# A decoder trunk on Trainium2: sixteen pairs of up strips, instead of ten, and one pair of gate strips with seven block products for eight

## The chip, the cores and the metric

The kernel runs on one core of a Trainium2 chip. The metric is the device time of one execution in microseconds (us). Engines are named as the profile names them: PE is the matrix engine and PEld its weight load, DVE the vector engine, ACT the scalar engine, POOL the general engine (here it issues the transfers that turn activations), and SP issues the loads of weights.

## The reference, cut to what matters

A trunk of two decoder layers over 256 tokens of width 2048, all in f32. Each layer has an attention mixer, a gated feed-forward part with a causal convolution of width 3, and a gate on a per-layer embedding:

```python
D_MODEL, SEQ, DEPTH = 2048, 256, 2
D_FF = 256 * ((8 * D_MODEL // 3 + 255) // 256)        # 5632
...
def conv_ffn(h, w_up, conv_w, conv_b, w_down):
    u = causal_depthwise_conv(h @ w_up, conv_w, conv_b)
    gate, val = u[..., :D_FF], u[..., D_FF:]
    return (jax.nn.silu(gate) * val) @ w_down
...
# per layer: h += mixer(norm(h)); h += conv_ffn(norm(h)); h += sigmoid(norm(h) @ w_gate) * (p[i] @ w_proj)
```

The up projection is 2048 by 11264 per layer, the down projection 5632 by 2048, the gate 2048 by 2048. With 256 tokens every weight is used for two blocks of 128 tokens.

## The kernel before, in words

**Strips and tiles.** A weight matrix is cut into strips of 512 columns; a strip is computed for both token blocks, each into one PSUM bank of 128x512. Weights arrive as `raw` tiles of 1 MB (128x2048, four blocks of 128x512), loaded on SP's queue into a pool of four (`NRAW`). An f32 block is multiplied as a high and a low part: ACT rounds a tile of two blocks to `whi` (L305), DVE subtracts to get `wlo` (L306), both in pools of four. Each block product is then three matmuls (`add_block`, L342 to L344): low activation by high weight, high by low, high by high. A tile of two blocks for two token blocks is 12 matmuls on PE.

**Seven products for eight.** The class `Seven` takes two strips together. Their first four blocks of 128 rows, two strips and two token blocks form a two by two product of block matrices, each block one tile of two weight blocks. Instead of eight tile products of 6 matmuls each it makes seven (the Strassen-Winograd scheme): `load` brings one raw tile of each strip, `first` to `fourth` make products 1 to 4, and then `fifth`, `sixth` and `seventh` the last three, which add to banks that already hold sums. Per pair it issues 6 matmuls fewer than the plain way. It issues three splits more (seven tiles for four, L464 on ACT and L465 on DVE), four additions of weights on DVE (L458), two copies out of PSUM on ACT (L494 and L502) and four sums in PSUM on DVE (L514 to L517). `block_sums` forms the sums of activations that the scheme needs, once for each set of activations. Its banks are c11, c12, c21 and c22; c11 and c21 belong to the first strip, c12 and c22 to the second.

**Where it stands.** The up projection of each layer is done in two parts; part 1 has pairs 0 to 4, part 2 pairs 5 to 10. A pair is a gate strip (columns of `gate`) and a value strip (columns of `val`), and the two strips of a pair are those of a Seven. Products 1 to 4 of a pair's Seven are put between the tiles of the value strip of the pair before (`begin`; this is called the head below), products 5 to 7 between the tiles of the pair's own first strip (`go_on`), and then the second strip follows (`end`). Before the change every second pair that could be a Seven is one: ten pairs in the two layers. A down projection follows each part, with a Seven for its strips 2 and 3 (four in all). So there are 14 Sevens.

**What follows an up strip.** The strip's two banks are scaled out of PSUM by ACT (`u`, L569), turned by DVE in blocks (L243) and by two transfers on POOL's queue through DRAM (`there`, L246, and `turned`, L254; this is called the turn chain below). One strip later ACT and DVE do the convolution on the turned strip (L935 on ACT, L938 to L944 on DVE); after a gate strip ACT takes SiLU, after a value strip DVE multiplies and splits into `g`, the activations of the down projection.

**What sets the order.** A scheduler places instructions on each engine in the order in which they are written, except that those under `tc.high_priority(offset=...)` (splits, weight additions, sums in PSUM) stand as many places earlier as the offset says, which was 200 for all (`AHEAD`). Each engine works its list in order. The order on each engine is thus known before a run.

The two functions that the change rewrites first, before it:

```python
def go_on(self):                       # tile hooks: product 5 ahead of tile 0, 6 ahead of 1, 7 ahead of 3
    hooks = dict(zip(TAILS, (self.fifth, self.sixth, self.seventh)))
    yield strip_among(self.W, self.strips[0], self.xs, hooks, [self.c11, self.c21], 4, self.base)
```

Of the kernel before, what the change touches and what calls it, by code (L numbers as in the profile page):

```python
# [50 lines left out]
HEADS, TAILS = {8: (1, 3, 5, 7), 6: (1, 2, 4, 5)}, (0, 1, 3)  # L51
# [19 lines left out]
AHEAD = 200  # L71
PI_PARTS = _two_pi_parts()
# [3 lines left out]
def tile_trunk(ctx, tc, head_d, xT_d, x_d, pT_d, pos_d, vec_d, cst_d, csb_d, wqkv, wo_a, wkv, wq_b, wo_b, wup, wdn, wpg, wpp, gfin_d, out_d):  # L76
# [184 lines left out]
    class Turned:  # L261
# [6 lines left out]
        def add(self, s):  # L268
            if self.strip is not None:
                with tc.issue_after(last["square"]), tc.issue_after(last["added"]):  # L270
                    self.use(*self.strip)
            self.strip = (s, turn(s))

        def late(self):
            self.use(*self.strip)

# [44 lines left out]
    def strip_v(W, s, xs, base=0, tail=2, ringed=0, begun=None, ends=True, before=lambda k0: None, room=None, halved=False, ready=None, hooks={}):  # L321
# [8 lines left out]
        for k, o, hi, lo in (g for group in it for g in group):  # L330
# [5 lines left out]
            add_block(ps[o], xs[k], min(o, 1), hi[:, c], lo[:, c], k == 0 and not begun, ends and k == n - 1)  # L336
# [22 lines left out]
    def products(jobs, xs, late=None, at=0, then={}, side=2, seven=None):  # L359
# [7 lines left out]
        if late is not None:  # L367
            n = len(xs)

# [4 lines left out]
            def before(k0):  # L374
                if k0 == at:
                    add()
                if k0 in then:
                    then[k0]()

            hooks = {}  # L380
            if seven is not None:
                tiles = n // 2
                hooks = {tiles - 4: seven.load, tiles - 2: seven.first, tiles - 1: seven.second}
            begun = [
                strip_v(
                    W,
                    s,
                    xs[:n],
                    base,
                    ends=False,  # L390
                    before=before if i == side - 1 else lambda k0: None,
                    room=two_banks() if i == 2 else None,
                    hooks=hooks if i == side - 1 else {},
                )
                for i, (W, s, base) in enumerate(jobs[:side])
            ]
# [5 lines left out]
            hooks = [{0: seven.third}, {0: seven.fourth}] if seven is not None else [{}] * side  # L402
            for b, (W, s, base), more in zip(begun, jobs, hooks):
                yield strip_v(W, s, xs[n:], base + n, begun=b, ready=ready, hooks=more)
                ready = None
            jobs = jobs[side:]
        if seven is not None:
            yield from seven.both()
            jobs = []
        for W, s, base in jobs:  # L410
            yield strip_v(W, s, xs, base)
# [25 lines left out]
    class Seven:  # L437
# [4 lines left out]
        def __init__(self, W, s0, s1, xs, sums, base=0, two=True):  # L442
            self.W, self.strips, self.base, self.two = W, (s0, s1), base, two
            self.xs, self.sums = xs, sums
# [4 lines left out]
        def value_bank(self, o):  # L449
            if not self.two:  # L450
                return bank("values", "acc")
            if o == 0:
                self.banks = two_banks()
            return self.banks[:, o]
# [29 lines left out]
        def first(self):  # L484
            self.c11 = bank("gates")
# [10 lines left out]
        def second(self):  # L496
            self.c12 = self.value_bank(0)
# [6 lines left out]
        def third(self):  # L504
            self.c21 = bank("gates", "acc")
            self.product(self.c21, self.sums[1], self.parts(self.u), True)

        def fourth(self):
            self.c22 = self.value_bank(1)
# [3 lines left out]
            with tc.high_priority(offset=AHEAD):  # L513
# [16 lines left out]

        def go_on(self):
# [3 lines left out]
        def end(self, hooks):  # L535
            return strip_among(self.W, self.strips[1], self.xs, hooks, [self.c12, self.c22], 4, self.base)

        def both(self):
            yield from self.go_on()
            yield self.end({})  # L540
# [681 lines left out]
```

## Time and profile before

| | before |
|---|---|
| three runs | 2280.93, 2282.38, 2282.47 us |
| median | 2282.38 us |
| the profiled execution, whole | 2284.18 us |
| its span in the profile | 2282.4 us |
| granted TensorE clock, mean | 0.998 |
| PE busy | 2267.6 us, 99% of the span |
| DVE busy | 1686.4 us, 74% |
| ACT busy | 1318.8 us, 58% |
| bytes moved | 538.44 MB, 236 GB/s |

A group of the profile stands as line, engine, operation, output and inputs, count, then busy time and mean duration of one. "Idle before" is time in which the engine waited ahead of that group, with what ended the wait. The number of a duration includes some overlap with the next instruction on the same engine, so the step from start to start is shorter than the duration. Instruction counts in the profile can be a few per cent lower than those issued.

### The profile page before, as it was taken

What the parts mean: (1) busy time and instruction counts of PE and PEld (TensorE: products, weight loads), DVE (VectorE), ACT (ScalarE), POOL (GpSimd) and SP (SyncE); (2) the same over time, 40 slices, a digit from 0 to 9 for tenths busy, and PEclk for the clock granted to TensorE, in tenths of its full rate; (3) what the DMA queues carried; (4) which work ended last, traced back from release to release, by engine and by line L of the source; (5) the groups of instructions that cost most, each with busy time, mean ns of one, the idle gap of its engine ahead of it and who ended that gap; (6) DMA issues with size and microseconds to landing.
All of it is one profiled execution on the core that took longest, in us unless ns stands there. A gap on an engine that the chain in (4) does not pass through costs nothing.

```text
span 2282.4 us, 28059 instructions
## 1 busy us (share of the span) xinstructions
PE 2267.6 (99%) x10113; PEld 1878.2 (82%) x10113; DVE 1686.4 (74%) x2471; ACT 1318.8 (58%) x1766; POOL 327.7 (14%) x575
## 2 busy tenths in 40 slices
PE   9999999999999999999999999999999999999998
PEld 7888888888888888888888888888888888888887
DVE  7656667688875888876667665768887588887665
ACT  6554555666644666655565554666664466665554
POOL 0211111111100111101111331211110011110100
PEclk9999999999999999999999999999999999999999
DMA  8777767676755767758676786767675576775863
GB/s 307 251 240 240 237 224 254 216 271 230 252 199 196 262 232 242 264 185 272 207 266 236 254 261 225 259 217 266 228 252 202 195 256 234 238 265 187 273 222 120
DMA packets 98348, 538.44 MB, mean 236 GB/s; under 512 B 16672, under 2 KB 17568, under 8 KB 46752
## 3 DMA queue, kind: packets, MB, share of 16 engines
q1 hardware_dynamic: 63360, 435.46, 54.6%
q0 software_dynamic: 32560, 95.98, 13.8%
q10 hardware_dynamic: 2288, 5.21, 0.6%
q8 instruction: 79, 1.29, 0.2%
q14 instruction: 61, 0.50, 0.1%
HBM read 486.52 MB, written 50.07 MB: 235 GB/s over the span
## 4 chain that ended last, share of the span: by engine, by line
PE 97%; DMA 2%; ACT 0%; POOL 0%; DVE 0%; issue 0%; POOLq 0%
PE accv L343 22%; PE accv L342 22%; PE accv L344 22%; PE two L343 4%; PE two L344 4%; PE two L342 4%; PE gates L343 4%; PE gates L344 4%; PE gates L342 4%; PE gates L474 3%; PE two L474 3%; PE two L583 1%; DMA turned<-there 1%; DMA there<-y 1%; PE keys L583 0%; POOL turned L254 0%
## 5 line engine op out<-in xcount | busy, mean ns | idle before, releaser
L306 DVE TENSOR_TENSOR wlo<-raw,whi 128x1024 fp32r<-128x1024 f32 (+1 forms) x768 | 931.5, 1215 | 455.2 <-ACT whi L305 452.7
L305 ACT ACTIVATE whi<-raw 128x1024 fp32r<-128x1024 f32 (+1 forms) x768 | 807.6, 1053 | 699.0 <-PE accv L344 426.1
L342 PE MATMUL accv<-whi,h 128*128 128x512 f32 (+1 forms) x1688 | 655.2, 388 | 2.4 <-DVE h L144 2.4
L344 PE MATMUL accv<-whi,h 128*128 128x512 f32 (+1 forms) x1688 | 656.3, 389 | 0.0
L343 PE MATMUL accv<-wlo,h 128*128 128x512 f32 (+1 forms) x1688 | 655.6, 388 | 0.0
L342 PEld LDWEIGHTS accv<-whi,h 128*128 128x128 f32 x1688 | 316.9, 188 | 68.6 <-DVE h L144 1.9
L343 PEld LDWEIGHTS accv<-wlo,h 128*128 128x128 f32 x1688 | 317.0, 188 | 65.8 <-DVE wlo L306 0.7
L344 PEld LDWEIGHTS accv<-whi,h 128*128 128x128 f32 x1688 | 317.0, 188 | 64.6
L246 POOL DMA_DIRECT2D there<-y x162 | 91.5, 565 | 1249.4 <-DVE y L243 1229.9
L254 POOL DMA_DIRECT2D turned<-there x324 | 189.5, 592 | 471.8 <-DMA there<-y 208.7
L464 ACT ACTIVATE whi<-raw 128x1024 fp32r<-128x1024 f32 x98 | 103.7, 1058 | 80.8 <-PE accv L344 68.2
L465 DVE TENSOR_TENSOR wlo<-raw,whi 128x1024 fp32r<-128x1024 f32 x98 | 119.8, 1222 | 34.8 <-ACT whi L464 34.5
L342 PE MATMUL accv<-whi,g 128*128 128x512 f32 x352 | 136.9, 389 | 0.0
L343 PE MATMUL accv<-wlo,g 128*128 128x512 f32 x352 | 136.9, 389 | 0.0
L344 PE MATMUL accv<-whi,g 128*128 128x512 f32 x352 | 136.9, 389 | 0.0
L342 PE MATMUL gates<-whi,h 128*128 128x512 f32 x240 | 93.4, 389 | 0.0
L343 PE MATMUL gates<-wlo,h 128*128 128x512 f32 x240 | 93.4, 389 | 0.0
L344 PE MATMUL gates<-whi,h 128*128 128x512 f32 x240 | 93.4, 389 | 0.0
L342 PE MATMUL two<-whi,h 128*128 128x512 f32 x240 | 93.4, 389 | 0.0
L343 PE MATMUL two<-wlo,h 128*128 128x512 f32 x240 | 93.4, 389 | 0.0
L344 PE MATMUL two<-whi,h 128*128 128x512 f32 x240 | 93.4, 389 | 0.0
L243 DVE STREAM_TRANSPOSE y<-u 128x512 f32<-128x512 f32 x122 | 84.1, 700 | 1.8 <-DMA there<-y 1.3
(224 smaller groups left out, 3024.2 us busy)
## 6 DMA issues: line engine op xcount, KB each, us to landing
raw<-in_wup SPq DMA_DIRECT2D x176, 1024.0 KB, 5.6
raw<-in_wdn SPq DMA_DIRECT2D x88, 1024.0 KB, 5.3
there<-y POOLq DMA_DIRECT2D x171, 256.0 KB, 5.2
turned<-there POOLq DMA_DIRECT2D x324, 128.0 KB, 5.1
raw<-in_wqkv SPq DMA_DIRECT2D x40, 1024.0 KB, 6.6
raw<-in_wpg SPq DMA_DIRECT2D x32, 1024.0 KB, 5.0
raw<-in_wkv SPq DMA_DIRECT2D x24, 1024.0 KB, 5.2
raw<-in_wo_a SPq DMA_DIRECT2D x16, 1024.0 KB, 5.4
```

Of the source, the lines that this page charges most:

```text
L243: last["turned"] = nc.vector.transpose(y.rearrange("p (b o r) -> p o b r", b=4, o=4), strip.rearrange("p (o b c) -> p o b c", o=4, b=4)).ins
L246: nc.gpsimd.dma_start(there[t * P : (t + 1) * P], y)
L254: nc.gpsimd.dma_start(z[32 * b : 32 * b + 32].rearrange("p a o r -> p a (o r)"), back[b])
L305: last["high"] = nc.scalar.activation(hi[:, c], r, AF.Copy).ins
L306: last["low weights"] = nc.vector.tensor_tensor(lo[:, c], r, f32(hi[:, c]), op=OP.subtract).ins
L342: nc.tensor.matmul(ps, xl, hi, start=first, stop=False, skip_group_check=again)
L343: nc.tensor.matmul(ps, xh, lo, start=False, stop=False, skip_group_check=again)
L344: nc.tensor.matmul(ps, xh, hi, start=False, stop=final, skip_group_check=again)
L464: last["high"] = nc.scalar.activation(hi, r, AF.Copy).ins
L465: last["low weights"] = nc.vector.tensor_tensor(lo, r, f32(hi), op=OP.subtract).ins
L474: nc.tensor.matmul(ps, x, y, start=begins, stop=ends, skip_group_check=True)
L583: run.append(nc.tensor.matmul(*args, skip_group_check=True, **kw).ins)
```

## The change

1. In the up projections every pair that follows another pair in its part is a Seven: pairs 2, 3, 4 (counted within part 1 from 0, the first two being plain in the way that the diff's condition gives) and all but the first of part 2. That makes 16 pairs for 10. Two Sevens now follow one another directly: the head of one stands in the value strip of another.
2. `go_on` has a new order. Before: product 5, tile 0 for both token blocks, product 6, tile 1, tile 2, product 7, the rest. Now: product 5, tiles 0 and 1 for c11, product 6, tiles 0 and 1 for c21, tile 2, product 7, the rest.
3. The four sums in PSUM are placed up to 400 places ahead (`SUMS_AHEAD`) instead of 200.
4. The banks are taken by tags that alternate from pair to pair: ("att", "two", "acc", "two") for one, ("att", "acc", "acc", "acc") for the next.
5. The gate of layer 0 (`wpg`) makes its strips 2 and 3 as a Seven: `load`, products 1 and 2 in strip 1's first pass, 3 and 4 as `PLAN_GATE` says. Its sums of activations are formed anew.

Other sites in the diff carry `False` (the queries, keys and values, `wo_a`, hosting a Seven in another projection) and change nothing. The diff, cut to its core:

```diff
+PLAN = {-4: "load", -2: "first", -1: "second"}, {0: "third"}, {0: "fourth"}
+PLAN_GATE = {-4: "load", -2: "first", -1: "second"}, {}, {0: "third", 1: "fourth"}
 AHEAD = 200
+SUMS_AHEAD = 2 * AHEAD
...
-        def __init__(self, W, s0, s1, xs, sums, base=0, two=True):
+        def __init__(self, W, s0, s1, xs, sums, base=0, banks=("att", "two", "acc", "two")):
...
+        def take(self, i):
+            if self.tags[i] != "two":
+                return bank("seven", self.tags[i])
+            self.two = self.two or two_banks()
+            return self.two[:, i // 2]
...
-            with tc.high_priority(offset=AHEAD):
+            with tc.high_priority(offset=SUMS_AHEAD):
                 nc.vector.tensor_tensor(self.p, self.c22, self.p, op=OP.add)
                 nc.vector.tensor_tensor(self.c21, self.c21, self.p, op=OP.add)
                 nc.vector.tensor_tensor(self.c22, self.q, self.c21, op=OP.subtract)
                 nc.vector.tensor_tensor(self.c12, self.c12, self.p, op=OP.subtract)
...
         def go_on(self):
-            hooks = dict(zip(TAILS, (self.fifth, self.sixth, self.seventh)))
-            yield strip_among(self.W, self.strips[0], self.xs, hooks, [self.c11, self.c21], 4, self.base)
+            xs, n = self.xs[4:], len(self.xs) - 4
+            ps = self.banks()[0]
+            it = weights(self.W, self.strips[0], n, base=self.base + 4)
+
+            def add(tiles, o):
+                for k0, hi, lo in tiles:
+                    for i in range(2):
+                        add_block(ps[o], xs[k0 + i], o, hi[i], lo[i], False, k0 + i == n - 1, True)
+
+            self.fifth()
+            tiles = [next(it) for _ in range(2)]
+            add(tiles, 0)
+            self.sixth()
+            add(tiles, 1)
+            for k, o, hi, lo in (g for group in steps(hooked(it, {1: self.seventh}), n, 2) for g in group):
+                add_block(ps[o], xs[k], o, hi, lo, False, k == n - 1, True)
+            return ps
...
-                    sums_next = j % 2 == (late is not None) and s + 1 in strips
-                    after = Seven(W, s + 1, v + 1, xs, sums) if sums_next else None
+                    v, final = s + FB // 4, s + 1 not in strips
+                    after = None
+                    if final and hosts:
+                        ...
+                    elif not final and (True and j or j % 2 == (late is not None)):
+                        after = Seven(W, s + 1, v + 1, xs, sums, 0, ("att", "two", "acc", "two") if j % 2 else ("att", "acc", "acc", "acc"))
...
-        gates = products([(wpg[i], s, 0) for s in range(3 if gain_of is None else 4)], xs, late, None)
+        seven = None
+        if True and gain_of is not None:
+            seven = Seven(wpg[i], 2, 3, xs, block_sums(xs[:4]), 0, ("att", "acc", "acc", "acc"))
+        jobs = [(wpg[i], s, 0) for s in range(3 if gain_of is None else 4)]
+        gates = products(jobs, xs, late, None, seven=seven, plan=PLAN_GATE)
```

Issued in the whole program, before and after: PE 9998 and 9956 instructions, DVE 2473 and 2564, ACT 1712 and 1749, POOL 579 both, SP 442 both.

The next rows are the lists of the engines as issued, in layer 0's up projection. Line numbers of the kernel before, L305 and L306 (split of a weight tile), L464 and L465 (split in a Seven), L569 (`u`), L935 (convolution on ACT), stand in the changed kernel as L320 and L321, L486 and L487, L609, L998. The first place is DVE at the begin of a Seven's own first strip, where the sums in PSUM stand. Before:

```order
L465 TENSOR_TENSOR wlo_7560<-raw_7329,whi_7559 128x1024
L306 TENSOR_TENSOR wlo_7572<-raw_7569,whi_7571 128x1024
L514 TENSOR_TENSOR part_7352<-two_7400,part_7352 128x512
L465 TENSOR_TENSOR wlo_7588<-raw_7329,whi_7587 128x1024
L515 TENSOR_TENSOR gates_7447<-gates_7447,part_7352 128x512
L243 STREAM_TRANSPOSE y_7528<-u_7523 128x4x4x32
L516 TENSOR_TENSOR two_7400<-part_7352,gates_7447 128x512
L306 TENSOR_TENSOR wlo_7598<-raw_7569,whi_7597 128x1024
L517 TENSOR_TENSOR two_7400<-two_7400,part_7352 128x512
L306 TENSOR_TENSOR wlo_7616<-raw_7613,whi_7615 128x1024
L243 STREAM_TRANSPOSE y_7531<-u_7525 128x4x4x32
```

Now, the same place:

```order
L321 TENSOR_TENSOR wlo_6498<-raw_6491,whi_6497 128x1024
L538 TENSOR_TENSOR two_6338<-part_6308,seven_6385 128x512
L487 TENSOR_TENSOR wlo_6514<-raw_6285,whi_6513 128x1024
L539 TENSOR_TENSOR two_6338<-two_6338,part_6308 128x512
L321 TENSOR_TENSOR wlo_6538<-raw_6535,whi_6537 128x1024
L155 TENSOR_TENSOR g_6268<-val_6248,g_6268 128x256
L155 TENSOR_TENSOR g_6269<-val_6248,g_6269 128x256
L155 TENSOR_TENSOR g_6270<-val_6248,g_6270 128x256
L155 TENSOR_TENSOR g_6271<-val_6248,g_6271 128x256
L247 STREAM_TRANSPOSE y_6450<-u_6445 128x4x4x32
L487 TENSOR_TENSOR wlo_6554<-raw_6287,whi_6553 128x1024
L247 STREAM_TRANSPOSE y_6453<-u_6447 128x4x4x32
```

Before, the first transpose (L243) stood between the second and the third sum, and one split ahead of the second transpose. Now both ordinary splits of the first load (the second is the first row shown) stand ahead of product 6's split (L487 of wlo_6514), and both transposes (L247) behind all four sums and the four parts of `g` (L155); the second transpose also stands behind the split of product 7 (L487 of wlo_6554).

The second place is DVE at the begin of a value strip. Before, where no Seven begins in it:

```order
L306 TENSOR_TENSOR wlo_7022<-raw_7003,whi_7021 128x1024
L306 TENSOR_TENSOR wlo_7040<-raw_7037,whi_7039 128x1024
L243 STREAM_TRANSPOSE y_6960<-u_6955 128x4x4x32
L306 TENSOR_TENSOR wlo_7056<-raw_7037,whi_7055 128x1024
L243 STREAM_TRANSPOSE y_6963<-u_6957 128x4x4x32
```

Now, with the head of the next Seven in it:

```order
L321 TENSOR_TENSOR wlo_6292<-raw_6289,whi_6291 128x1024
L487 TENSOR_TENSOR wlo_6310<-raw_6285,whi_6309 128x1024
L321 TENSOR_TENSOR wlo_6323<-raw_6289,whi_6322 128x1024
L480 TENSOR_TENSOR raw_6285<-raw_6285,raw_6287 128x1024
L247 STREAM_TRANSPOSE y_6242<-u_6237 128x4x4x32
L480 TENSOR_TENSOR raw_6287<-raw_6287 128x1024
L487 TENSOR_TENSOR wlo_6340<-raw_6285,whi_6339 128x1024
L247 STREAM_TRANSPOSE y_6245<-u_6239 128x4x4x32
L480 TENSOR_TENSOR raw_6285<-raw_6285,raw_6287 128x1024
L321 TENSOR_TENSOR wlo_6354<-raw_6351,whi_6353 128x1024
```

Between the strip's splits there now stand the Seven's two splits (L487) and its additions (L480) as well as the two transposes.

The third place is ACT in a value strip. Before, without a head in it:

```order
L305 ACTIVATE whi_7039<-raw_7037 128x1024
L569 ACTIVATE u_6955<-gates_6615,rcol_3055 128x512
L305 ACTIVATE whi_7055<-raw_7037 128x1024
L569 ACTIVATE u_6957<-gates_6711,rcol_3055 128x512
L935 ACTIVATE val_6966<-turned_6818,vec 128x256 x3
L305 ACTIVATE whi_7073<-raw_7071 128x1024
L935 ACTIVATE val_6966<-turned_6818,vec 128x256
```

Now, with a head in it:

```order
L320 ACTIVATE whi_6667<-raw_6665 128x1024
L486 ACTIVATE whi_6685<-raw_6661 128x1024
L320 ACTIVATE whi_6698<-raw_6665 128x1024
L609 ACTIVATE u_6613<-seven_6307,rcol_3055 128x512
L609 ACTIVATE u_6615<-seven_6385,rcol_3055 128x512
L998 ACTIVATE val_6624<-turned_6476,vec 128x256 x3
L486 ACTIVATE whi_6715<-raw_6661 128x1024
L320 ACTIVATE whi_6729<-raw_6727 128x1024
L998 ACTIVATE val_6624<-turned_6476,vec 128x256
```

Three convolutions that read `turned_6476` still stand together behind the scaling of the strip before; behind them now waits the split for product 2 of the Seven's head (L486).

More of the change, by code (lines that the diff above doesn't have):

```diff
@@ L401, in products @@
                 add()
-            hooks = [{0: seven.third}, {0: seven.fourth}] if seven is not None else [{}] * side
-            for b, (W, s, base), more in zip(begun, jobs, hooks):
-                yield strip_v(W, s, xs[n:], base + n, begun=b, ready=ready, hooks=more)
+            for b, (W, s, base), more in zip(begun, jobs, later):
+                yield strip_v(W, s, xs[n:], base + n, begun=b, ready=ready, hooks=more, again=bool(first))
                 ready = None
             jobs = jobs[side:]
[L407 to L411, printed above, removed]
+        if seven:
+            yield seven.go_on()
+            yield seven.end(host())
+            return
+        for i, (W, s, base) in enumerate(jobs):
+            after = host() if i == len(jobs) - 1 else None
+            yield strip_v(W, s, xs, base, hooks=after.begin(len(xs) // 2) if after else {})
     def block_sums(xs):
@@ L717, in mixer_a @@
         nc.vector.tensor_scalar(rq, rc, QS, None, op0=OP.mult)
-        q, k, ws, os = {}, {}, {}, []
+        q, k, ws, os, vs = {}, {}, {}, [], []
+        sums = block_sums(xs[:4]) if False else None
+        pair = [None]
         def turned(which, g, ps=None):
+            if ps is None and pair[0]:
+                ps = pair[0].end() if which else pair[0].go_on()
             us = scaled(ps or strip_v(wqkv, 4 * which + g, xs), (rq, rc)[which], ring_room)
@@ L911, in add_strips, with hosted @@
         turned = Turned(use)
-        seven = Seven(W, 2, 3, xs, block_sums(xs[:4]), base) if gain_of is None or base else None
-        for s, ps in enumerate(products([(W, s, base) for s in range(4)], xs, late, at, side=side, seven=seven)):
+        begun = [None]
+        def hosted():
+            if host is not None:
+                begun[0] = host(out)
+            if seven and norm is not None and not base:
+                return turned
+            return begun[0]
+        jobs = [(W, s, base) for s in range(4)]
+        for s, ps in enumerate(products(jobs, xs, late, at, {}, side, first, seven, plan, hosted)):
             if norm is not None and s == 3:
@@ L920, in add_strips, with ffn @@
             if norm is not None:
-                turned.add(s)
-        return out, turned.late
-    def ffn(i, xs, late, rc):
+                turned.add(s, seven and not base and s == 2)
+        return out, turned.late, begun[0]
+    def ffn(i, xs, late, rc, began):
         cv = V_CONV + i * 4 * 2 * FB
@@ L944, in conv_turned, with part @@
                 nc.vector.tensor_tensor(c, c, over, op=OP.add)
-        def part(strips, late=None):
+        def part(strips, late=None, hosts=False):
             gs = []
             gate = [None]
-            sums = block_sums(xs)
+            down = [None]
+            sums = began.sums if began and late is not None else block_sums(xs)
             def finish_strip(value, s, z):
@@ L980, in up_strips @@
                     else:
-                        yield from now.go_on()
-                        yield now.end(after.begin(6) if after else {})
+                        yield now.go_on()
+                        yield now.end(after)
                     now = after
```

134 lines of the change are left out of this document (87 added, 47 removed).

## The prediction

> **What bounds the kernel now.** I read the page's busy shares and its chain first, then what PE waits for, then single stretches of an up projection.
>
> ```profile
> span 2282.4 us, 28059 instructions
> ...
> PE 2267.6 (99%) x10113; PEld 1878.2 (82%) x10113; DVE 1686.4 (74%) x2471; ACT 1318.8 (58%) x1766; POOL 327.7 (14%) x575
> ...
> PE 97%; DMA 2%; ACT 0%; POOL 0%; DVE 0%; issue 0%; POOLq 0%
> ```
>
> PE is the bound: 99% busy and 97% of the chain that ended last. What it waits for, from the view of waits:
>
> ```profile
> PE accv L342 <- DVE h L144: 2.4, 2, 1.4
> PE two L583 <- DMA turned<-there: 1.3, 1, 1.3
> PE warm L125 <- DVE zero L122: 1.2, 1, 1.2
> ```
>
> The columns are us in total, times, longest. The largest is 2.4 us in two waits, so waits between matmuls hold nothing to win; a kernel with fewer matmuls gains what they take, so long as PE goes on being fed. Now the price of a matmul. The two timeline rows are the first matmuls of product 5 in two Sevens of layer 0's part 2, two pairs apart; the window rows give us, then busy time (count) of PE, PEld, DVE, ACT and POOL, the granted clock, the DMA share and GB/s. The first window is the end of a plain value strip with a head in it, the second the two pairs between those matmuls.
>
> ```profile
> 471.41 0.39 PE L474 MATMUL gates<-whi,h 128*128 128x512 f32 x1
> 557.09 0.39 PE L474 MATMUL gates<-whi,h 128*128 128x512 f32 x1
> 446.90:471.40 24.50, 24.50 (x109) 20.28 (x108) 24.01 (x35) 15.40 (x21) 3.47 (x6) 1.00 0.61 215
> 471.40:557.10 85.70, 85.70 (x380) 70.97 (x379) 72.82 (x110) 54.57 (x71) 13.89 (x24) 1.00 0.72 246
> ```
>
> Two pairs hold 2 x 192 - 6 = 378 matmuls, and 85.68 us between the two rows makes 0.2267 us each. PE is busy without a gap at a clock of 1.00.
>
> The Trainium skill, "TensorE: Matmul & The Clock Gate", section "Back-to-back issue gap", gives about 131 ns for a matmul of 512 columns in a sustained stream. Here the trace says 227 ns and decides. By the page's figure 42 matmuls would be worth an estimated 5.5 us, and the same stalls as below would then leave the time about 1.7 us above before.
>
> **Matmuls removed.** PE issues 9998 - 9956 = 42 fewer: seven more Sevens by 6. 42 x 0.2267 = 9.52 us (six up pairs 8.16, the gate 1.36). This comes off PE's path in full.
>
> **Work added to DVE and ACT.** Each Seven adds on DVE 3 splits, 4 additions of weights and 4 sums in PSUM, on ACT 3 splits and 2 copies.
>
> ```profile
> 556.05 1.22 DVE L465 TENSOR_TENSOR wlo<-raw,whi 128x1024 fp32r<-128x1024 f32 x1
> 557.18 0.69 DVE L515 TENSOR_TENSOR gates<-gates,part 128x512 f32<-128x512 f32 x1
> 557.78 0.70 DVE L243 STREAM_TRANSPOSE y<-u 128x512 f32<-128x512 f32 x1
> 558.41 0.67 DVE L516 TENSOR_TENSOR two<-part,gates 128x512 f32<-128x512 f32 x1
> 558.98 1.20 DVE L306 TENSOR_TENSOR wlo<-raw,whi 128x1024 fp32r<-128x1024 f32 x1
> ...
> L458 DVE TENSOR_TENSOR raw<-raw 128x1024 f32<-128x1024 f32 x28 | 34.3, 1225 | 0.9
> L464 ACT ACTIVATE whi<-raw 128x1024 fp32r<-128x1024 f32 x98 | 103.7, 1058 | 80.8 <-PE accv L344 68.2
> L465 DVE TENSOR_TENSOR wlo<-raw,whi 128x1024 fp32r<-128x1024 f32 x98 | 119.8, 1222 | 34.8 <-ACT whi L464 34.5
> L502 ACT ACTIVATE part<-two 128x512 f32<-128x512 f32 x14 | 8.4, 600 | 4.2 <-PE two L474 4.2
> ```
>
> From start to start a split takes 1.13 us, a sum 0.60, a transpose 0.63; an addition lasts as long as a split (1225 against 1222 ns). So a Seven costs DVE 3 x 1.13 + 4 x 1.13 + 4 x 0.60 = 10.3 us, and ACT at most 3 x 1.06 + 2 x 0.60 = 4.4. In the second window one of the two pairs is a Seven. With both, DVE has 72.8 + 10.3 = 83.1 us of work in 85.68 - 1.36 = 84.3 (99%), ACT 59.0 (70%). On average it fits, by 1.2 us: nothing for the sums and additions themselves, since they lie beside PE's own stream. The first window shows DVE 98% busy while PE ran on. But a queue that full recovers no lateness, so I look where PE's next need comes soonest.
>
> There are 12 places where the head of a Seven stands in the value strip of a pair that is itself a Seven: 2 in part 1 and 4 in part 2, by two layers. I put time 0 at product 5. PE then runs 18 + 72 = 90 matmuls in the first strip (20.4 us) and 72 + 24 = 96 in the second (21.8).
>
> **Place 1, the first tile of the value strip.** PE needs its high half at 20.4 and its low half at 20.6. Two of the four raw buffers are held by the Seven's own two loads, so the other six loads of a pair pass through two, where a plain pair has four.
>
> ```profile
> raw<-in_wup SPq DMA_DIRECT2D x176, 1024.0 KB, 5.6
> ...
> ACT whi L305 <- DMA raw<-in_wup: 22.0, 10, 3.3
> ...
> 802.35 1.06 ACT L305 ACTIVATE whi<-raw 128x1024 fp32r<-128x1024 f32 x1 [3.28 <-DMA raw<-in_wup]
> ```
>
> The strip's first load takes the buffer of tiles 2 and 3. DVE's list puts tile 3's split behind the second transpose, which ends about 9.9 (place 2 tells why), so the buffer comes free at 9.9 + 1.13 = 11.0. A median load of 5.6 us lands at 16.6; one that is late by the longest wait shown, 3.3 us, at 19.9. ACT waited for such loads ten times before. High and low take 1.06 + 1.22, so the low half is ready at 18.9 or 22.2: early by 1.7 us or late by 1.6. In six of the twelve a transpose and an addition (0.63 + 1.13 us) stand ahead of that split on DVE; with the median load it is then ready at 20.7, 0.1 late. Bounds for one place: 0 (a tile that is early can't make PE earlier) and 1.6; I take 0.3, nearer to the median load. 12 x 0.3 = 3.6 us.
>
> **Place 2, the convolution on ACT ahead of product 2's split.** In six of the twelve (the second in part 1, the second and fourth in part 2, by two layers) three convolutions of the strip before stand ahead of L486 for product 2. They wait for the turn chain; behind them on ACT are this split, the next tile's and PE.
>
> ```profile
> L246 POOL DMA_DIRECT2D there<-y x162 | 91.5, 565 | 1249.4 <-DVE y L243 1229.9
> L254 POOL DMA_DIRECT2D turned<-there x324 | 189.5, 592 | 471.8 <-DMA there<-y 208.7
> ...
> there<-y POOLq DMA_DIRECT2D x171, 256.0 KB, 5.2
> turned<-there POOLq DMA_DIRECT2D x324, 128.0 KB, 5.1
> ...
> 476.16 0.70 DVE L243 STREAM_TRANSPOSE y<-u 128x512 f32<-128x512 f32 x1
> 493.61 1.57 ACT L935 ACTIVATE val<-turned,vec 128x256 f32<-128x256 f32 x3
> ...
> 561.84 0.70 DVE L243 STREAM_TRANSPOSE y<-u 128x512 f32<-128x512 f32 x1
> 581.76 1.59 ACT L935 ACTIVATE val<-turned,vec 128x256 f32<-128x256 f32 x3 [2.38 <-DMA turned<-there]
> 583.25 1.05 ACT L305 ACTIVATE whi<-raw 128x1024 fp32r<-128x1024 f32 x1
> ```
>
> Before, the second transpose ended at 562.54, 5.5 us behind product 5 (557.09). Now it stands behind the split for product 7. PE frees that split's weight buffer after tile 0, for c21, at about 6.8 to 8.2 us; high, low and transpose put its end near 9.9. From there the chain takes at least 0.57 + 5.2 + 4 x 0.59 + 5.1 = 13.2 us by the medians. The two chains shown took at most 16.75 (476.86 to 493.61, where ACT did not wait) and 19.2 (562.54 to 581.76, where it did). The turned strip is there at 23.1, 26.7 or 29.1. Product 2 starts at 20.4 + 12 + 6 + 12 matmuls = 27.2, its low half is due at 27.4, and three convolutions (1.5), high (1.0) and low (1.2) need 3.7 ahead of it: no stall for a strip that lands by 23.7. So PE is early by 0.6, or late by 3.0 or 5.4. Before, the 2.38 us on ACT cost PE nothing, as no head waited behind. I take 14.4 for the chain, 0.6 late, nearer to the medians, since 16.75 only bounds the first chain from above. 6 x 0.6 = 3.6 us.
>
> **The rest.** The order of `go_on` moves matmuls and removes none; c21 is now wanted 2.7 us later than before, while the four sums move ahead of it, so no stall. The four down projections have no head in them. The banks of alternate tags are freed by `u` one strip before they are taken. SP and POOL issue as much as before, and the same bytes. In the gate of layer 0 one Seven more meets slack:
>
> ```profile
> 1100.00:1125.00 25.00, 25.00 (x112) 20.72 (x111) 13.05 (x14) 12.02 (x14) 0.00 (x0) 1.00 0.56 186
> ```
>
> DVE is 52% busy there, 12 us free in 25; the 10.3 us and the sums of activations fit in two strips. I cost it at nothing; its bounds are 0 and the 1.4 us that it gains, beyond which a stall would show as a wait of a size that no row of that stretch has.
>
> **The sum.** -9.5 + 3.6 + 3.6 = -2.3 us. On the profiled span of 2282.4 that is 2280.1, on its execution 2284.18 it is 2281.9; that execution lies 1.8 us (0.08%) above the median of 2282.38, from which I get 2280.1. I predict 2280. With both places at nothing it is 2272.9, with both at their ends 12 x 1.6 + 6 x 3.0 - 9.5 = +27.7, 2310.1.
>
> **The rivals.** (a) The covers hold: loads land as the median and the chain takes 13.2. Then at most 0 to 4.8 us is lost, 2273 to 2277.7, about 2275. For it speaks that PE lost nothing with DVE at 98% in the first window; against it the convolutions that already waited 2.38 us in the row of 581.76.
>
> (b) Slower, by the turn chain alone: at 16.75, as in the first chain's bound, place 2 costs 6 x 3.0 = 18, and with place 1 at 3.6 the sum is +12, 2294. It decides from the point where place 2 takes more than 1.75 us each (-9.5 + 3.6 + 10.5 = +4.6), that is a chain over 15.6 us. For it speaks the 19.2 us chain; against it that the first chain ended without a wait.
>
> (c) PE idles so long that its clock drops: a chain of 19.2 in three of the six makes gaps of 5.4 us.
>
> ```profile
> 1.20 3.83 PE L125 MATMUL warm<-zero 128*128 128x512 bf16 x9 [1.20 <-DVE zero L122]
> ```
>
> At the start, with the clock low, nine matmuls took 3.83 us, 0.43 each for 0.23; a drop costs 9 x 0.2 = 1.8 us again. Then 3 x (5.4 + 1.8) + 3 x 3.0 + 3.6 - 9.5 = +24.7, 2307. The longest wait of PE in the rows above is 1.4 us, which shows no drop. The Trainium skill, same page, section "HAM oscillation — how this bites in real kernels", puts the limit at PE gaps of about 3.4 us; no run here shows it yet.
>
> **How the numbers follow.** What tells a change of this kernel from none is about 0.2%, 4.6 us (2277.8 to 2286.9). My own forecast, stalls between 4.9 and 14 us, has 0.42; (a) 0.36; (b) 0.20; (c) 0.02. So faster 0.36, same 0.42, slower 0.22. The range leaves out (c), the upper part of (b) and all below 2273, no more than 2 in 10: 2273 to 2290; the likeliest case alone 2278 to 2286.
>
> **What the changed profile would show.** PE about 9.5 us less busy; 12 gaps of at most 1.6 us ahead of a value strip's first tile, ended by `wlo` or `whi` of L320 and L321; six ahead of product 2, with ACT's convolution (L998) waiting for `turned` in front. If ACT doesn't wait there, (a) is right; if each gap exceeds 1.75 us, (b). Wrong altogether would be a stall at product 6 or in the gate, or a DVE that is late in every strip.

## The result, and the profile after

The changed kernel takes 2306.1 us (median of four runs, 2296.7 to 2308.8) against 2282.4 before: the ratio is 1.0095, 95% interval 1.0083 to 1.0107. That is 23.7 us slower, where 2280 had been forecast and 2273 to 2290 given as the range. The profiled execution of the changed kernel took 2303.6 us, its span 2301.7.

The page's head, the chain and what PE waits for, of the changed kernel:

```profile
span 2301.7 us, 28134 instructions
...
PE 2269.4 (99%) x10071; PEld 1868.6 (81%) x10071; DVE 1752.9 (76%) x2562; ACT 1339.9 (58%) x1803; POOL 328.7 (14%) x575
...
PE 74%; DVE 13%; DMA 7%; issue 3%; ACT 1%; POOL 1%; ACTq 0%; DVEq 0%; POOLq 0%
```
```profile
PE seven L358 <- DVE wlo L321: 6.5, 9, 0.9
PE two L358 <- DVE wlo L321: 4.5, 6, 0.8
PE seven L357 <- ACT whi L320: 3.3, 3, 2.2
PE accv L357 <- DVE h L148: 2.3, 2, 1.5
...
PE seven L496 <- DVE wlo L487: 1.1, 2, 0.6
```

The matmuls went as counted (42 fewer), and PE still counts as 99% busy. But PE's part of the chain fell from 97% to 74%, with DVE and the DMA in its place, and the list of PE's waits is no longer that of before: PE waits for `wlo` and `whi` in the up projections. The busy share hides this: in these records a matmul lasts 0.39 us and the next starts 0.227 us after it, so a delay of up to 0.16 us leaves no gap. So I measured each step from one matmul of 512 columns to the next in the trace, took 0.227 us off it and summed what is left by the tile that PE was about to start:

| PE late at | before | after |
|---|---|---|
| start of the program and before the first Seven | 6.5 | 6.7 |
| first tile of a value strip that holds a head | 0 | 15.2 |
| tile behind product 2 | 0 | 3.9 |
| product 6 | 0 | 3.7 |
| tile 1 of a Seven's first strip | 0 | 2.4 |
| product 2 | 0 | 0.9 |
| elsewhere | 3 | 4 to 5 |
| all | 9.5 | 37 to 38 |

About 28 us of new lateness less 9.5 us of matmuls is 18 to 19; the two spans differ by 19.3. So this table holds nearly the whole result.

The largest item has a simple picture. These are rows of the changed kernel's timeline round one value strip in layer 0's part 2, whose Seven began at 842.71 (SP's rows are issues of 1 MB loads, L502 the next Seven's own two and L303 those of the strip), and two windows:

```profile
847.30 0.33 SPq L502 DMA_DIRECT2D raw<-in_wup  x1
852.02 0.33 SPq L502 DMA_DIRECT2D raw<-in_wup  x1
853.49 0.33 SPq L303 DMA_DIRECT2D raw<-in_wup  x1
857.55 0.33 SPq L303 DMA_DIRECT2D raw<-in_wup  x1
...
864.84 1.06 ACT L320 ACTIVATE whi<-raw 128x1024 fp32r<-128x1024 f32 x1 [8.38 <-DMA raw<-in_wup]
...
865.95 0.50 PE L357 MATMUL seven<-whi,h 128*128 128x512 f32 x1 [2.23 <-ACT whi L320]
867.21 0.50 PE L358 MATMUL seven<-wlo,h 128*128 128x512 f32 x1 [0.76 <-DVE wlo L321]
...
842.70:863.50 20.80, 20.65 (x91) 16.63 (x89) 17.69 (x31) 10.38 (x16) 5.06 (x9) 1.00 0.93 289
867.30:870.90 3.60, 3.60 (x10) 2.81 (x11) 3.60 (x4) 3.60 (x7) 0.00 (x0) 0.61 0.18 32
```

The load that holds the strip's first tile is the third in SP's queue. It was issued at 853.49, 10.8 us behind product 5, and landed 11.2 us later. The load before it, the one after it and the turned strip's transfers ran beside it, and the DMA engines were 93% busy over 20.8 us, at 289 GB/s. At the twelve such places of this trace that load starts 9.5 to 11.3 us behind product 5 and takes 7.3 to 11.2 us (8.7 at the median); loads with little beside them take about 5. ACT stood idle 8.4 us for it, and PE started the tile 2.4 us late by its steps, then waited another 1.0 us for the low half. The last window shows what followed in this one place: a mean clock of 0.61.

### The profile page after: what moved, and what is told of

It is laid out like the page before. It is cut to its first block, busy times and chain, and to the rows that moved or that the text cites. A ratio compares the mean times of both kernels' runs of the same rounds, so it can differ in the third digit from the quotient of the medians.

```text
span 2301.7 us, 28134 instructions
## 1 busy us (share of the span) xinstructions
PE 2269.4 (99%) x10071; PEld 1868.6 (81%) x10071; DVE 1752.9 (76%) x2562; ACT 1339.9 (58%) x1803; POOL 328.7 (14%) x575
## 4 chain that ended last, share of the span: by engine, by line
PE 74%; DVE 13%; DMA 7%; issue 3%; ACT 1%; POOL 1%; ACTq 0%; DVEq 0%; POOLq 0%
PE accv L358 17%; PE accv L357 17%; PE accv L359 17%; DVE wlo L321 4%; PE seven L358 4%; PE seven L359 4%; PE seven L357 4%; PE seven L496 3%; DVE wlo L487 3%; DMA raw<-in_wup 2%; DMA there<-y 2%; PE two L358 2%; PE two L357 2%; PE two L359 2%; DMA turned<-there 2%
## 5 line engine op out<-in xcount | busy, mean ns | idle before, releaser
L321 DVE TENSOR_TENSOR wlo<-raw,whi 128x1024 fp32r<-128x1024 f32 (+1 forms) x740 | 894.8, 1213 | 408.0 <-ACT whi L320 405.3
L320 ACT ACTIVATE whi<-raw 128x1024 fp32r<-128x1024 f32 (+1 forms) x740 | 776.4, 1052 | 635.9 <-PE accv L359 372.7
L357 PE MATMUL accv<-whi,h 128*128 128x512 f32 x1240 | 480.9, 388 | 2.3 <-DVE h L148 2.3
L359 PE MATMUL accv<-whi,h 128*128 128x512 f32 x1240 | 482.0, 389 | 0.0
L358 PE MATMUL accv<-wlo,h 128*128 128x512 f32 x1240 | 481.3, 388 | 0.0
L357 PEld LDWEIGHTS accv<-whi,h 128*128 128x128 f32 x1240 | 232.8, 188 | 51.0 <-ACT whi L320 2.0
L358 PEld LDWEIGHTS accv<-wlo,h 128*128 128x128 f32 x1240 | 232.8, 188 | 48.1 <-DVE wlo L321 0.7
L359 PEld LDWEIGHTS accv<-whi,h 128*128 128x128 f32 x1240 | 232.9, 188 | 47.5
L358 PE MATMUL seven<-wlo,h 128*128 128x512 f32 x624 | 244.5, 392 | 6.5 <-DVE wlo L321 6.5
L357 PE MATMUL seven<-whi,h 128*128 128x512 f32 x624 | 243.7, 390 | 3.3 <-ACT whi L320 3.3
L359 PE MATMUL seven<-whi,h 128*128 128x512 f32 x624 | 243.6, 390 | 0.0
L486 ACT ACTIVATE whi<-raw 128x1024 fp32r<-128x1024 f32 x147 | 155.4, 1057 | 116.3 <-PE accv L359 46.2
L487 DVE TENSOR_TENSOR wlo<-raw,whi 128x1024 fp32r<-128x1024 f32 x147 | 178.8, 1217 | 34.7 <-ACT whi L486 34.4
L358 PEld LDWEIGHTS seven<-wlo,h 128*128 128x128 f32 x624 | 117.4, 188 | 34.6 <-DVE wlo L321 10.5
L357 PEld LDWEIGHTS seven<-whi,h 128*128 128x128 f32 x624 | 117.4, 188 | 29.1 <-ACT whi L320 4.5
L359 PEld LDWEIGHTS seven<-whi,h 128*128 128x128 f32 x624 | 117.5, 188 | 24.1
L247 DVE STREAM_TRANSPOSE y<-u 128x512 f32<-128x512 f32 x122 | 84.6, 700 | 3.3 <-DMA there<-y 1.7
```

Of the source, the lines that this page charges most:

```text
L247: last["turned"] = nc.vector.transpose(y.rearrange("p (b o r) -> p o b r", b=4, o=4), strip.rearrange("p (o b c) -> p o b c", o=4, b=4)).ins
L320: last["high"] = nc.scalar.activation(hi[:, c], r, AF.Copy).ins
L321: last["low weights"] = nc.vector.tensor_tensor(lo[:, c], r, f32(hi[:, c]), op=OP.subtract).ins
L357: nc.tensor.matmul(ps, xl, hi, start=first, stop=False, skip_group_check=again)
L358: nc.tensor.matmul(ps, xh, lo, start=False, stop=False, skip_group_check=again)
L359: nc.tensor.matmul(ps, xh, hi, start=False, stop=final, skip_group_check=again)
```

## The experiments

Three theories stand behind them. A: a value strip's first load stands behind the next Seven's two loads in SP's queue and is late. C: DVE is simply too full. E: DVE has time enough, but its list puts work ahead of the splits that PE needs. B, D and F to I are rivals named with each run. The kernels were timed in four groups, each on another chip and beside the kernel before, whose median was between 2281.8 and 2282.6 us in each group; the ratios are to that. Line numbers shift by a few between kernels.

**Ten pairs with all else of the change but the alternate banks.** Edit:

```diff
-                    elif not final and (True and j or j % 2 == (late is not None)):
-                        after = Seven(W, s + 1, v + 1, xs, sums, 0, ("att", "two", "acc", "two") if j % 2 else ("att", "acc", "acc", "acc"))
+                    elif not final and j % 2 == (late is not None):
+                        after = Seven(W, s + 1, v + 1, xs, sums, 0, ("att", "two", "acc", "two"))
```

> The changed kernel with every second pair as a Seven again (ten pairs, no Seven directly behind another), and with all else that it brought: the new order at a Seven's begin, the sums further ahead, the gate's Seven. Theory A (the loss comes from Sevens that follow one another: the next Seven's two loads stand in SP's queue ahead of the value strip's first load, and it lands late): no such places are left, so 2282.4 - 1.4 for the gate = 2281, between 2279 and 2283. Rival B (the new order and the sums ahead make the stalls, wherever a Seven begins): ten of the sixteen places stay, so about 2282 + 0.6 x 28 - 1.4 = 2297.

Measured: 2280.4 us against 2281.8, ratio 0.9993 (0.9984 to 1.0002). No PE wait between matmuls in the up projections; its whole list is

```profile
PE accv L357 <- DVE h L148: 1.2, 1, 1.2
PE warm L129 <- DVE zero L126: 1.2, 1, 1.2
```

So the new order, the sums further ahead and the gate's Seven cost nothing by themselves (the 1.3 us fit the gate's 1.36, within the interval of no change). The loss needs Sevens that follow one another, or the alternate banks that come with them; the last kernel but one below has both and is faster than the kernel before, so the banks alone are not it. Rival B falls.

**Sixteen pairs with the old order at a Seven's begin.** Edit: `go_on` as before, `SUMS_AHEAD = AHEAD`.

> The changed kernel with sixteen pairs and the gate's Seven, but with the old order at a Seven's begin (product 5, tile 0, product 6) and the sums in PSUM 200 places ahead. Theory A: the loads keep their order, so the stalls ahead of the value strip's first tile stay (about 15 us with what follows from them); 2300 to 2312. Rival B: the stalls go with the order, about 2275 to 2283.

Measured: 2302.5 us, 1.009 (1.0076 to 1.0104). The number is A's, the way to it is not. The sum by tiles is 16.5 us at tile 0 for c21, where PE waits for the sum in PSUM, and only 1.8 at the value strip's first tile:

```profile
PE seven L357 <- DVE seven L538: 8.5, 6, 1.8
PE seven L357 <- DVE two L538: 4.7, 6, 1.2
```

A first strip that loses 1.4 us (16.5 us over twelve places) gives the late load 1.4 us more. The load also landed somewhat earlier here, 16.7 to 19.2 us behind product 5 at the twelve places against 17.2 to 22.0 in the changed kernel; why is not shown. So the new order does remove a wait (PE meets c21 six matmuls, 1.4 us, later), and about as much was lost at the next tile that was due. A number that fits is no proof of a mechanism.

**The Seven's loads behind the strip's first load.** Edit, in the changed kernel:

```diff
-            return {0: self.load, **dict(zip(HEADS[tiles], ...
+            return {-1: self.load, **dict(zip(HEADS[tiles], ...
...                                    # in hooked(), behind next(it):
+            if i == 0 and -1 in hooks:
+                hooks[-1]()
```

> The changed kernel with one edit: in a strip that holds the head of a Seven, the Seven's two loads stand behind that strip's first load in SP's queue instead of ahead of it. Theory A: the strip's first load starts about 6 us earlier, at +4.6 instead of +10.8 behind product 5, and lands by +11, 7 us before it must; the stalls there (14.7 us in the profile, one clock drop among them) go, and with them those of the tile behind product 2 (3.8 us), which I read as their echo on DVE: 2306 - 18 = 2288, between 2284 and 2292. Rival C (DVE is simply too full in a pair that follows another, the load only looks like the cause): the stall moves to another tile, 2300 or more. Rival D (place 2 is the wait for the turned strip, not an echo): its 3.8 us stay, about 2291.

Measured: 2288.5 us, 1.0031 (1.0021 to 1.0041), 17.6 us less than the changed kernel, 18 were expected. The value strip's first tile is never late any more. In the place that answers to the one shown, product 5 is at 836.72:

```profile
842.30 0.33 SPq L303 DMA_DIRECT2D raw<-in_wup  x1
846.91 1.46 SPq L502 DMA_DIRECT2D raw<-in_wup  x2
```

The strip's load starts at +5.6 instead of +10.8 and lands after 5.1 us. The Seven's two follow; PE needs the first 2.7 us and the sum that takes in the second 6.8 us behind the strip's first tile. The long landing is now that of the second, 11.2 us, which has the most time. Theory A is shown for this part. The tile behind product 2 is late by 1.7 us in all instead of 3.9, so most of that was an echo. But the loss at product 6 grew from 3.7 to 9.2 us. There DVE works without a gap and PE waits for it:

```profile
835.05 1.42 DVE L155 TENSOR_TENSOR g<-val,g 128x256 fp32r<-128x256 f32 x4
836.40 1.22 DVE L321 TENSOR_TENSOR wlo<-raw,whi 128x1024 fp32r<-128x1024 f32 x1
837.53 0.68 DVE L536 TENSOR_TENSOR part<-seven,part 128x512 f32<-128x512 f32 x1
838.13 1.21 DVE L321 TENSOR_TENSOR wlo<-raw,whi 128x1024 fp32r<-128x1024 f32 x1
839.26 0.69 DVE L537 TENSOR_TENSOR seven<-seven,part 128x512 f32<-128x512 f32 x1
839.87 0.69 DVE L539 TENSOR_TENSOR seven<-seven,part 128x512 f32<-128x512 f32 x1
840.46 0.68 DVE L538 TENSOR_TENSOR seven<-part,seven 128x512 f32<-128x512 f32 x1
841.06 1.22 DVE L487 TENSOR_TENSOR wlo<-raw,whi 128x1024 fp32r<-128x1024 f32 x1
...
841.29 0.47 PE L496 MATMUL seven<-whi,h 128*128 128x512 f32 x1 [0.33 <-DVE seven L538]
842.33 0.50 PE L496 MATMUL seven<-wlo,h 128*128 128x512 f32 x1 [0.56 <-DVE wlo L487]
```

**Two sums behind product 6's split.** Edit, on top of the last: the sums for c22 and c12 are written behind `self.sixth()`. In this kernel the sum for c22 reads c21 with product 6 already in it, so what it computes differs from the reference.

> As the kernel with the Seven's loads behind the strip's first load, and with the last two of the four sums in PSUM (those for c22 and c12) put behind product 6's split on DVE instead of ahead of it. In the changed kernel's profile DVE runs without a gap there and product 6's low half is 0.25 to 0.81 us late at eight places (4.3 us in all), tile 1's low half 1.1 us at two (2.4). Theory A: the two sums take 1.2 us of DVE's time ahead of these splits, so about 6 us more go: about 2282, between 2278 and 2286. Rival C: no gain beyond the other edit's.

Measured: 2297.0 us, 1.0065 (1.0052 to 1.0077), 8.5 us slower than without. A sum that reads c21 behind product 6 puts DVE between two writers of one bank on PE: in this trace PE waits 8.5 us in all, in twelve waits, for that sum. So this says nothing on the cost of the list. Only the sum for c12 may go behind.

**Work taken off DVE by POOL.** On top of the loads behind: the low parts of `g` on POOL; or one weight addition of each Seven; or both, with the sum for c12 behind product 6's split; or the last with the loads as in the changed kernel. Edits: `nc.gpsimd.tensor_tensor` for `nc.vector.tensor_tensor` in these places.

> As the kernel with the Seven's loads behind the strip's first load, and the four low parts of g (1.34 us of DVE per pair, which stand ahead of product 5's and product 6's splits) computed on POOL. What is left in that kernel's profile is 8.2 us ahead of product 6, where DVE works without a gap for over 10 us, and 4 us elsewhere. Theory E (what is left comes from DVE's list being full just there): 1.34 us less ahead of product 6 takes away all of its 0.5 to 1.3 us at eight places: 2288.5 - 8 = 2280, between 2277 and 2284. Rival F (the sums wait for PE's product 4 or for their operands, not for DVE's time): no change, 2286 to 2291. Rival G (POOL's work on SBUF slows DVE, or holds up the turn chain that POOL issues): 2290 or more.

> As the kernel with the Seven's loads behind the strip's first load, and one of the four additions of weights of each Seven (1.13 us of DVE, at the head in the value strip) computed on POOL. Theory E: DVE's list has no gap from the head to product 6, so 1.13 us less anywhere in it makes product 6 earlier by nearly as much: 2288.5 - 7 = 2281, between 2278 and 2285. If the list does have gaps between, only the 2.7 us at the tile behind product 1 go: 2286. Rival G: slower than 2290.

> Both of these together (low parts of g and one addition on POOL, the Seven's loads behind the strip's first load), and the sum for c12 always behind product 6's split. 2.5 us less for DVE in 42 per pair. Theory E: no stalls are left in the up projections but about 1 us, so 2282.4 - 9.5 + 1 = 2274, between 2272 and 2277: faster than before. Rival F: 2286 to 2291. Rival G: over 2280.

> The same work on POOL and the same place of the sum for c12, but with the Seven's two loads ahead of the value strip's first load, as in the changed kernel. Theory A (two separate causes, the late load and DVE's full list): the 14.7 us ahead of the value strip's first tile stay, or a little more, since PE now comes there earlier; 2274 + 15 = 2289, between 2285 and 2300. Rival C (DVE's full list is the one cause, also of the late load, because DVE's splits free the raw buffers): 2274 to 2279.

Measured, in this order: 2300.9 (1.0082, 1.0068 to 1.0095), 2300.4 (1.0080, 1.0066 to 1.0094), 2310.2 (1.0125, 1.0111 to 1.0138) and 2338.8 us (1.0252, 1.0228 to 1.0276). All far slower than the 2288.5 without: rival G. With the addition on POOL:

```profile
L514 POOL TENSOR_TENSOR raw<-raw 128x1024 f32<-128x1024 f32 x21 | 65.5, 3118 | 408.2 <-DVE raw L480 303.2
...
865.65 3.17 POOL L514 TENSOR_TENSOR raw<-raw 128x1024 f32<-128x1024 f32 x1 [8.97 <-DVE raw L480]
...
866.48 0.71 DVE L247 STREAM_TRANSPOSE y<-u 128x512 f32<-128x512 f32 x1
867.10 2.80 DVE L487 TENSOR_TENSOR wlo<-raw,whi 128x1024 fp32r<-128x1024 f32 x1
```

POOL needs 3.1 us for what DVE does in 1.13, and DVE's split beside it took 2.80 us for 1.22, so DVE gets back 1.13 us and pays 1.6 in this place. The split was held up rather than slowed: at all 21 places the split that starts while POOL adds ends 1.08 us after POOL does, whether it took 1.80 or 3.38 us by that, while the transpose shown, which reads one tile, kept its 0.7 us. (The Trainium skill, "GPSIMD Engine Reference", section "1. Specifications", lists the SBUF interfaces as shared, with contention against DVE instructions that read two SBUF inputs; these rows agree.) These four runs don't tell E from H, and the fourth, meant to tell A from C, has both costs in it.

**Work moved behind product 6 on DVE.** On top of the loads behind, nothing is taken off DVE; the sum for c12 and the four parts of `g` are written behind product 6's split:

```diff
             self.sixth()
+            self.last_sum()                                  # c12 - p
+            with tc.issue_after(last["low weights"]):
+                self.then()                                  # g of the pair before
             add(tiles, 1)
```

> As the kernel with the Seven's loads behind the strip's first load, with no work taken off DVE but moved: the four parts of g (1.34 us of DVE, needed only by the down projection) are written behind product 6 of the next pair instead of ahead of it (DVE's list then has them at that strip's end), and the sum for c12 stands behind product 6's split. Theory E (DVE has enough time in a pair, 83 of 84 us in two, and loses only by what its list puts ahead of product 6): the 8.2 us ahead of product 6 go: 2288.5 - 8 = 2280, between 2277 and 2284. Rival H (DVE is full over the pair as a whole, so the same time is lost at the next tile that is due): no change, 2286 to 2291.

Measured: 2283.3 us (12 runs, 2276.0 to 2291.0), 1.0002 (0.9991 to 1.0013): 5 us less, of 8 expected, though the ranges of the two kernels overlap (2285.5 to 2292.4 without). Of product 6's 9.2 us, 7.5 are left in its profile; at six of the seven places the list has a transpose among the sums ahead of product 6's split.

**Additions behind the next tile's split.**

> As that kernel, and the head's first two additions of weights stand behind the next tile's split on DVE instead of ahead of it, so that this split no longer waits with them for the Seven's second load (the profile of the kernel with the loads behind shows DVE waiting 14 us for that load in all, and 2.7 us of PE at the tile behind product 1). Theory E: 2.7 us less than the kernel before it, about 2277, between 2274 and 2282. Rival H: 2286 to 2291.

Measured: 2290.2 us, 1.0029 (1.0018 to 1.0040), 7 us slower than the kernel before it, a miss. With the additions moved, the scheduler also put `val` by `gate` (1.14 us) directly ahead of the first sum, and PE was 0.2 to 0.3 us late at tiles 0 and 1 and product 6 of nearly every Seven. The largest item lies elsewhere: the tile behind product 2 lost 7.1 us in its profile, where the kernel before it lost 3.7, while product 6 lost only 3.1. The two effects were not taken apart.

**The transposes behind product 6's split too.** On top of the kernel with `g` behind: the next pair's products 5 and 6 are written ahead of the strip's turn, and the turn is bound to stand behind.

```diff
-                        yield now.go_on()
-                        yield now.end(after)
+                        yield now.go_on(True)
+                        ps = now.end(after)
+                        if after:
+                            after.then = flush
+                            after.start()                    # products 5 and 6, tiles 0 and 1
+                        yield ps
...
-                    there = turn_out(scaled(next(ups), rc, room))
+                    us = scaled(next(ups), rc, room)
+                    with tc.issue_after(last["sixth"]) if "sixth" in last else ExitStack():
+                        there = turn_out(us)
```

> As the kernel with the Seven's loads behind the strip's first load and with g written behind product 6, and now the two transposes of the strip before (0.63 us each) also stand behind product 6's split, at all sixteen pairs. What is left ahead of product 6 on DVE is what must be there: the splits of product 5 and of tiles 0 and 1, three sums, its own. Theory E (what is lost ahead of product 6 is lost by what DVE's list puts there): the 7.5 us that the kernel before it still loses ahead of product 6 go, 2283.3 - 7 = 2276, between 2273 and 2280, faster than before. Rival H (DVE is full over the pair, the time is lost at the next tile that is due): 2281 to 2288. Rival I (the transposes come 1 to 3 us later, so ACT's convolution waits for the turned strip, with product 2 behind it, as the prediction had it): up to 12 x 2 us at product 2, 2285 or more.

Measured: 2274.8 us (2274.2 to 2278.1) against 2282.6, ratio 0.9969 (0.9957 to 0.9981): faster than both kernels, and where E put it. What PE waits for, DVE's list ahead of product 6, and a window over two steady pairs:

```profile
PE accv L357 <- ACT whi L320: 2.4, 1, 2.4
PE warm L129 <- DVE zero L126: 1.2, 1, 1.2
PE seven L497 <- DVE wlo L488: 0.8, 2, 0.6
PE accv L357 <- DVE h L148: 0.4, 1, 0.4
...
836.23 0.69 DVE L538 TENSOR_TENSOR seven<-seven,part 128x512 f32<-128x512 f32 x1
836.96 0.70 DVE L539 TENSOR_TENSOR seven<-part,seven 128x512 f32<-128x512 f32 x1
837.56 1.22 DVE L488 TENSOR_TENSOR wlo<-raw,whi 128x1024 fp32r<-128x1024 f32 x1
838.70 0.69 DVE L543 TENSOR_TENSOR seven<-seven,part 128x512 f32<-128x512 f32 x1
839.30 1.21 DVE L321 TENSOR_TENSOR wlo<-raw,whi 128x1024 fp32r<-128x1024 f32 x1
840.43 1.42 DVE L155 TENSOR_TENSOR g<-val,g 128x256 fp32r<-128x256 f32 x4
841.77 1.30 DVE L247 STREAM_TRANSPOSE y<-u 128x512 f32<-128x512 f32 x2
...
835.27:919.59 84.32, 84.32 (x373) 69.82 (x372) 82.67 (x121) 58.70 (x76) 13.89 (x24) 1.00 0.73 254
```

84.32 us for two pairs is 372 matmuls of 0.2267, without a gap, while DVE is busy 82.67 of them (98%). So a DVE this full is no bound here; rival H falls, and so does I, since nothing waits at product 2 although the transposes come later (the second starts 4.9 to 9.0 us behind product 5, in the kernel before 4.7).

**The same list with the loads as in the changed kernel.** Edit: `{-1: self.load` back to `{0: self.load`.

> The same list order on DVE, but with the Seven's two loads ahead of the value strip's first load, as in the changed kernel: this leaves only the late load. Theory A: the first load of the value strip starts at +10.8 and lands at +18 to +22 as in the changed kernel, PE loses 1 to 3.4 us ahead of that tile at most of the twelve places, 15 to 20 us in all: 2276 + 17 = 2293, between 2286 and 2302. Rival C (with DVE's list in order the raw buffers come free earlier and the load lands in time): 2273 to 2281.

Measured: 2300.2 us, 1.0075 (1.0062 to 1.0087), at the upper end of what A expected; C falls. The lateness by tiles is 17.5 us at the value strip's first tile, 5.3 behind product 2 and 3.3 at product 6, where the same list with the loads behind has 0, 0 and 1.6:

```profile
PE seven L358 <- DVE wlo L321: 7.0, 10, 0.8
...
PE two L357 <- ACT whi L320: 2.8, 2, 2.1
PE two L358 <- DVE wlo L321: 2.6, 4, 0.8
PE seven L357 <- ACT whi L320: 2.1, 4, 0.7
```

So the two causes are separate, and the load is the larger: 25 us between these two kernels. Their sizes do not add, though. With the load late, the list's order is worth about 6 us (2306.1 to 2300.2, and the ranges of the two kernels overlap); with the loads in order it is worth 14 (2288.5 to 2274.8). The late load hides most of what the list costs; how, no run shows.

## Why the prediction was wrong, point by point

- **The step that failed most.** On the profiled span 2280.1 had been worked out and 2301.7 were measured, 21.6 more. Place 1 gives 11.6 of it (15.2 for 3.6): the duration of the value strip's first load was mis-sized. The tile behind product 2, product 6 and tile 1, which stood in the sum at nothing, give 3.9, 3.7 and 2.4. Place 2 gives back 2.7, and some 2 us lie elsewhere.
- **The gain.** 42 matmuls for 9.5 us was right: two pairs take 84.32 us once nothing waits, and 84.3 had been worked out.
- **DVE on average.** 83.1 us of work in 84.3 was right (82.67 in 84.32), and so was the reading that the average settles nothing. What failed is the step that cost the sums and the additions at nothing, and the sums ahead of c21 with "no stall": the places that I worked through were the value strip's first tile and product 2, and product 6 was left out, though the list of DVE ahead of its split was known and a stall there had been named as the sign of being wrong altogether. Nor is c21 wanted 2.7 us later than before: it is six matmuls, 1.4 us. Ahead of that split the list holds what is needed later: in the changed kernel a fourth sum or the end of the convolution with `val` by `gate`, in the later kernels also `g` or a transpose. That cost 3.7 us there and 2.4 at tile 1 in the changed kernel, and 9.2 at product 6 with the loads in order.
- **Place 1 was the right place and mis-sized.** 3.6 us were taken, 12 x 1.6 = 19 given as its bound; 15.2 were measured, at eight of the twelve places, none in part 1. The load's start was right (11.0, measured 10.8). The term that failed is its duration: I took the median of 5.6 us from the page of the profile, which mixes loads with little and with much beside them, and bounded it by the longest wait of ACT before, 3.3 us more. It took 8.7 at the median of the twelve places and 11.2 in the place shown, where other loads and a turn chain ran beside it; 3.4 us were lost there, over the bound of 1.6. The trace of before held the answer, which I passed by: at all ten Sevens of its up projections the load issued 8.1 us behind product 5 takes 10.4 to 12.1 us. And I took SP's order as given, where the Seven's two loads ahead of the strip's own are the cause.
- **Place 2 was not one.** 3.6 us were forecast at product 2 and rival (b) hung on it; in the changed kernel PE lost 0.9 us at product 2, in three places, and 0.5 at most, though ACT's convolution of `val` (L998) did wait for `turned`, 12.3 us in nine waits. The 3.9 us at the tile behind it mostly go with the late load, and later transposes cost nothing in the kernel at 2274.8. So (b), which forecast 2294, gave the right direction for a wrong reason.
- **Rival (c) happened, at another place and at a smaller gap than it needs.** Behind the 2.23 us wait with 0.76 after it, at a value strip's first tile and not at product 2, the granted clock had a mean of 0.61 over 3.6 us. Seven matmuls took 0.43 us each and two a little less: 1.6 us, where 1.8 had been worked out. In the last kernel above, waits of 2.09 and 0.76 us did the same (0.60 over 4 us), and in the changed kernel waits of 0.67 and 0.77 us did not. That the 0.43 us at the program's start were a low clock, no row of before shows (its granted clock there reads 1.00); here they stand beside one. The Trainium skill, "TensorE: Matmul & The Clock Gate", section "HAM oscillation — how this bites in real kernels", puts the limit at gaps over about 3.4 us; here the two waits together are 3.0 us, with one matmul between.
- **The gate** cost nothing, as forecast: no wait there in the kernel with ten pairs.

## What to carry to other kernels

Where loads pass through a small pool in one queue, order them by when each is needed, not by when its user appears in the program, and take a load's duration from the rows in which as many others run beside it. An engine at 98% need not cost its neighbour anything: what counts is what its list puts ahead of each result that the bound engine is about to need, so move to behind it what is needed late. When a fix only moves the lateness to the next tile that is due, count the lateness by tile before judging it.

## What the runs showed of the hardware that was not expected

An f32 addition of 128x1024 took POOL 3.1 us and DVE 1.22, and a DVE split of the same size that started beside it ended 1.08 us after POOL did at all 21 places, so that it took 1.80 to 3.38 us instead of 1.22. Loads of 1 MB that land after about 5 us with little beside them took up to 11.2 in the changed kernel with other loads and a turn chain beside them, at a DMA share of 0.93 and 289 GB/s. The granted clock fell for some 3.4 us after PE waits of 2.23 and 0.76 us with a single matmul between them.
